# One hybrid decoder layer on one core: split remainders shared with GpSimd, a native first row, loaded bias tables, a new order

## The chip, the cores and the metric

The kernel runs on one core of a Trainium2 chip. The metric is the device time of one execution in microseconds, as the median of several runs. Three runs of the kernel before took 236.06, 235.83 and 234.94 us, so the median is 235.83 us. TensorE (PE) multiplies matrices and transposes, VectorE (DVE), ScalarE (ACT) and GpSimd (POOL) work on elements, and SyncE (SP) issues nearly all DMAs.

## The reference, cut to what matters

One layer of 256 tokens and 1024 channels. One projection by `w_in` (1024 x 5906) feeds four groups of six heads of width 64; each group's output is multiplied by its own SiLU gate; the four are joined, projected by `w_out` (1536 x 1024), and merged with a layer norm.

```python
proj = x @ w_in                       # split into the four groups' columns
y_a = moba_attention(a_q, a_k, a_v, slopes_moba) * silu(a_g)   # at 256 tokens: causal softmax with ALiBi
xbc = silu(causal_dw_conv(s_xbc))
y_b = rms_norm(ssd_mixer(xbc, s_dt, ...) * silu(s_z))          # Mamba-2 scan, dt = softplus(...)
y_c = dilated_attention(c_q, c_k, c_v, slopes_dil) * silu(c_g)
qkv = silu(causal_dw_conv(d_qkv))                              # q, k normalised
o_d = gated_delta_chunked(q, k, v, sigmoid(d_b), -exp(A) * softplus(d_a + bias))
y_d = rms_norm(o_d) * silu(d_g)
mix = concat([y_a, y_b, y_c, y_d]) @ w_out
out = layer_norm(2 ** 0.25 * x + mix)
```

## The kernel before

**Projections.** Every float32 weight tile is split (`split`, line 418) into a rounded part `whi` (ACT, float32r) and a remainder `wlo` = raw - whi (a subtraction on DVE, or on POOL where the running number of the split is in `POOL`, line 75: only number 6). The activations are split once into `xhi` and `xlo` (lines 469 to 472). A product is then three float32r matmuls, hi by hi, hi by lo and lo by hi, in this order within a tile, so the remainder is wanted last. There are 62 splits: 4 of the leading tiles `lead`, 46 of further `w_in` tiles and 12 of `w_out`. Tiles `raw`, `whi` and `wlo` have four buffers each, and SP issues the loads of `raw` in one queue. `channels` (line 495) computes columns with channels on partitions, `tokens` (517) with tokens on partitions, and `first_channels` (506) the first 512 columns while the input is still arriving, row block by row block, from `lead`.

**Stages.** The delta group comes first: conv k, gate d, `decays`, norm k, conv q, products `M` and `A`, conv v. Its triangular blocks are inverted on DVE by 62 small instructions on `Ub` (lines 785 to 789), whose results pass through DRAM; then join and delta. Beside it run gate s, conv bc, conv x, state and scan of the Mamba group, and the two attentions c and a. The output projection and the layer norm in two halves of 128 tokens come last. In `attention` (626), DVE adds a bias table to the scores and takes the maximum of a row, a small instruction multiplies it by -0.125 (line 646), and ACT takes the exponential with it as bias. DVE makes the table `biasc` (line 935) and ACT makes `biasa` (line 942), six instructions each, from loaded distances in `csb`. `softplus` (549) runs twice, once for each group.

**The order** of all instructions on all engines is written out by a planner in the kernel (class `Plan`): every call is recorded with an estimated cost, and a list scheduler picks the next by the length of the way to the end plus a priority of its stage (`PRIO`). `LIMIT` says how many of the eight PSUM banks a kind of use may hold. The engine wrapper gives DVE and POOL work on SBUF a shared resource `port`. All instructions are recorded at one helper line (356), so the profile tells them apart by tiles. Waits follow from the data.

Of the kernel before, what the change touches and what calls it, by code (L numbers as in the profile page):

```python
# [13 lines left out]
OP = mybir.AluOpType  # L14
# [41 lines left out]
NEAR = CAT["moba"][0]  # L56
# [4 lines left out]
SWITCH, PORT, AHEAD = 0.17, 0.9, {"dve": 0.015, "pe": 0.185}  # L61
# [5 lines left out]
PRIO = {"split": -6.8, "conv k": 1086.3, "gate d": -51.1, "decay d": 1000.2, "norm k": 1627.6, "conv q": 1480.8,  # L67
        "products": 1504.1, "norm q": 1768.9, "gate s": 323.3, "decay s": -1394.4, "values c": 263.3,
        "conv v": 246.6, "blocks": 124.5, "join": -297.8, "delta": 975.5, "conv bc": -546.4, "conv x": -369.3,
        "state": 595.2, "scan": 1273.9, "scores c": -1234.3, "attention c": 2093.1, "scores a": -183.7,  # L70
        "values a": -1630.5, "attention a": -481.0, "out": 94.7, "out 0": -1157.7, "out 1": -1399.5,
        "ln 0": -2309.4, "ln 1": 877.3}
CONST = -5, -4, -3
NRAW = 4
POOL = (6,)
POOLS = {"ps": (8, 512, F), "work": (3, W, F), "workd": (2, W, F), "workx": (1, W, F), "workg": (2, W, F), "cy": (3, S, F), "p": (3, W, F), "mx": (3, 4, F), "pt": (3, W, F), "oss": (2, 6, F), "sss": (2, 1, F), "srs": (2, 1, F)}
RINGS = {"raw": 4, "whi": 4, "wlo": 4}
LIMIT = {"pj": 5, "g": 6, "ed": 1, "es": 5, "n": 6, "m": 4, "d": 4, "o": 1, "td": 5, "b": 2, "s": 2, "ts": 4, "c": 6, "ct": 5, "cv": 6, "a": 4, "at": 1, "av": 1}
BEGIN, SLOW = 1.2, 2.5


class Plan:
# [69 lines left out]
    def add(self, eng, call, cost, outs, ins, dma=0.0, mode=None, port=False, place=None, slow=0.0):  # L152
# [5 lines left out]
        op = {"id": i, "bias": self.bias, "stream": self.stream, "eng": eng, "call": call, "cost": cost, "dma": dma,  # L158
# [41 lines left out]
    def run(self):  # L200
# [48 lines left out]
        while len(order) < len(ops):  # L249
# [22 lines left out]
            cost = o["cost"] * (0.5 if o["mode"] and o["mode"] == mode and o["place"] != place else 1.0)  # L272
# [94 lines left out]
def hybrid_layer(ctx, tc, plan, xT, x, w_in, w_out, convw, small, ln_g, ln_b, cst, out):  # L367
# [64 lines left out]
    rows, first, rest = [(slice(k, k + 1), slice(0, 512)) for k in range(2)], slice(0, 256), slice(256, 512)  # L432
    ws_lead = [split(w, rows if n else [(rows[0][0], first), (rows[0][0], rest), rows[1]]) for n, w in enumerate(lead)]
# [61 lines left out]
    def channels(c0, n):  # L495

        for j in range(n // 128):
            hi, lo = split(load(w_in, 0, KC, c0 + j * 128, 128))
            b = bank("pj")
            for n in range(3 * KC):  # L500
                p, k = n // KC, n % KC
                pj.matmul(b[:, :S], (lo if p == 2 else hi)[:, k, :], (xlo if p == 1 else xhi)[:, k, :],
                          start=n == 0, stop=n == 3 * KC - 1)
            yield j, b[:, :S]

    def first_channels():

        bs = [bank(t) for t in ("pj", "pj", "pj", "a")]
        for k in range(KC):
            hi, lo = ws_lead[k // 2]  # L510
            for p in range(3):
                for j in (0, 3, 1, 2):
                    pj.matmul(bs[j][:, :S], (lo if p == 2 else hi)[:, k % 2, (j * 128 + 128) % 512:][:, :128],
                              (xlo if p == 1 else xhi)[:, k, :], start=(k == 0 and p == 0), stop=(k == KC - 1 and p == 2))
        yield from enumerate(b[:, :S] for b in bs)

    def tokens(c0, n, raw=(), kinds=("pj", "pj")):

# [9 lines left out]
        for i in range(2):  # L528
            yield i, bs[i]
# [90 lines left out]
    def scores(m, cols, tag):  # L620
        qk[m] = new(m + "qk", 2, 3, S, tag=tag)
        for n in range(2):
            for j, b in channels(cols[n], W):
                act.activation(qk[m][:, n, j, :], b, AF.Copy)

    def attention(m, k0, bias, tag):
# [5 lines left out]
        for pr in range(3):  # L632

            ss, pts = [bank(m) for _ in halves], []
# [4 lines left out]
            for e, s_ in enumerate(ss):  # L639
                h = 2 * pr + e  # L640
                p, mx = new("p", W), new("mx", 2, 2)
# [16 lines left out]
                pts.append(pt)  # L658
            b = bank(m + "v")
# [85 lines left out]
    part("gate s")  # L745
    gz, raws = new("gz", 2, W), new("raws", 2, 6)
    for i, b in tokens(S_Z, NZ):
        gate(gz[:, i, :], b)
        dve.tensor_copy(raws[:, i, :], b[:, W:NZ])
    sdv, dt, sda = new("sdv", 2, 6), new("dt", 2, 6), new("sda", 2, 6)  # L750
    dve.tensor_add(sdv, raws, P("sdt")[:, None, :].to_broadcast([128, 2, 6]))
    softplus(sdv, dt)
    dve.scalar_tensor_tensor(sda, dt, -1.0, expA[:, 0:1, :].to_broadcast([128, 2, 6]), op0=OP.mult, op1=OP.mult)
# [64 lines left out]
    for i in range(2):  # L818
# [6 lines left out]
        for r in range(2):  # L825
            tp = slice(64 * r, 64 * r + 64)
# [11 lines left out]
        if i == 0:  # L838
# [95 lines left out]
    for h in range(NH):  # L934
        dve.scalar_tensor_tensor(bc[:, h, :], C("dil"), float(8 * SLOPES[h]), C("lnc"), op0=OP.mult, op1=OP.add)
# [5 lines left out]
    for h in range(NH):  # L941
        act.activation(ba[:, h, :], C("moba"), AF.Copy, scale=float(8 * SLOPES[6 + h]))
# [122 lines left out]
```

## Time and profile before

| what | us |
|---|---|
| median of three runs | 235.83 |
| the profiled execution | 235.13 |
| its span in the trace | 233.40 |
| PE busy | 221.6 |
| PE loading weights | 198.2 |
| DVE busy | 178.6 |
| ACT busy | 142.2 |
| POOL busy | 22.3 |

The profiled execution's time is 1.73 us longer than its span. A matmul's record covers its whole passage through the array, and the next one starts long before it ends, so PE can look busy across a short bubble. The row of weight loads (PEld) shows such bubbles better, as each matmul here has a load of its own.

### The profile page before, as it was taken

What the parts mean: (1) busy time and instruction counts of PE and PEld (TensorE: products, weight loads), DVE (VectorE), ACT (ScalarE), POOL (GpSimd) and SP (SyncE); (2) the same over time, 40 slices, a digit from 0 to 9 for tenths busy, and PEclk for the clock granted to TensorE, in tenths of its full rate; (3) what the DMA queues carried; (4) which work ended last, traced back from release to release, by engine and by line L of the source; (5) the groups of instructions that cost most, each with busy time, mean ns of one, the idle gap of its engine ahead of it and who ended that gap; (6) DMA issues with size and microseconds to landing.
All of it is one profiled execution on the core that took longest, in us unless ns stands there. A gap on an engine that the chain in (4) does not pass through costs nothing.

```text
span 233.4 us, 4547 instructions
## 1 busy us (share of the span) xinstructions
PE 221.6 (95%) x1679; PEld 198.2 (85%) x1679; DVE 178.6 (77%) x448; ACT 142.2 (61%) x300; POOL 22.3 (10%) x26
## 2 busy tenths in 40 slices
PE   7999999999999999899999999899999999999970
PEld 3999999699998999899888889697889988877870
DVE  2876999898869998899999996542579865464275
ACT  4777684656782544944669387999955547352210
POOL 3023020300020000000000000000023320000071
PEclk9999999999999999999999999999999999999997
DMA  6999627987550198666923524750525507550013
GB/s 177 357 368 325 186 84 200 272 215 212 144 152 14 18 262 237 172 183 179 260 79 81 145 73 128 192 161 4 176 94 183 179 4 246 204 180 3 0 67 113
DMA packets 45957, 36.92 MB, mean 158 GB/s; under 512 B 5600, under 2 KB 42592, under 8 KB 45936
## 3 DMA queue, kind: packets, MB, share of 16 engines
q1 hardware_dynamic: 45504, 36.25, 53.6%
q10 hardware_dynamic: 432, 0.39, 0.5%
q8 instruction: 13, 0.21, 0.3%
q14 instruction: 8, 0.07, 0.1%
HBM read 35.00 MB, written 1.64 MB: 157 GB/s over the span
## 4 chain that ended last, share of the span: by engine, by line
PE 42%; DVE 30%; DMA 11%; ACT 9%; issue 4%; SPq 2%; DVEq 0%; ACTq 0%
PE ps L356 42%; DVE wlo L356 10%; DMA raw<-in_w_in_dram 10%; DVE Ub L356 5%; DVE cy L356 4%; ACT whi L356 2%; DMA lead<-in_w_in_dram 2%; SPq L356 2%; DVE p L356 1%; DVE M L356 1%; DVE A L356 1%; ACT p L356 1%; ACT Ed L356 1%; DVE r L356 1%; ACT Tb L356 1%
## 5 line engine op out<-in xcount | busy, mean ns | idle before, releaser
L356 ACT ACTIVATE whi<-raw 128x1024 fp32r<-128x1024 f32 (+3 forms) x57 | 56.9, 1001 | 37.5 <-PE ps L356 25.6
L356 DVE TENSOR_TENSOR wlo<-raw,whi 128x1024 fp32r<-128x1024 f32 (+3 forms) x56 | 64.1, 1153 | 18.1 <-ACT whi L356 15.5
L356 PE MATMUL ps<-xhi,whi 128*128 128x256 f32 x272 | 42.0, 287 | 0.2 <-ACT whi L356 0.2
L356 PE MATMUL ps<-xhi,wlo 128*128 128x256 f32 x272 | 41.2, 285 | 0.0
L356 PE MATMUL ps<-xlo,whi 128*128 128x256 f32 x272 | 41.1, 285 | 0.0
L356 PEld LDWEIGHTS ps<-xhi,whi 128*128 128x128 f32 x272 | 35.8, 189 | 3.1 <-ACT whi L356 1.4
L356 PEld LDWEIGHTS ps<-xhi,wlo 128*128 128x128 f32 x272 | 35.7, 189 | 0.7 <-issue 0.7
L356 PEld LDWEIGHTS ps<-xlo,whi 128*128 128x128 f32 x272 | 35.7, 189 | 0.6 <-DVE xlo L356 0.2
L356 PE MATMUL ps<-whi,mix 128*128 128x512 f32 (+1 forms) x110 | 28.4, 349 | 0.0
L356 ACT ACTIVATE p<-p,mx 128x256 f32<-128x256 f32 (+1 forms) x48 | 19.6, 442 | 4.7 <-DVE mx L356 4.6
L356 PEld LDWEIGHTS ps<-whi,mix 128*128 128x128 f32 x110 | 19.2, 188 | 2.8
L356 DVE SCALAR_TENSOR_TENSOR cy<-ps,cw,cy 128x253 f32<-128x253 f32 (+2 forms) x48 | 19.9, 477 | 0.9 <-ACT cy L356 0.9
L356 PE MATMUL ps<-wlo,mix 128*128 128x512 f32 (+1 forms) x55 | 19.1, 353 | 0.0
L356 PE MATMUL ps<-whi,xlo 128*128 128x384 f32 (+2 forms) x64 | 17.6, 346 | 0.0
L356 PE MATMUL ps<-wlo,xhi 128*128 128x384 f32 (+2 forms) x64 | 17.1, 344 | 0.0
L356 PE MATMUL ps<-whi,xhi 128*128 128x384 f32 (+2 forms) x64 | 17.1, 345 | 0.0
L356 PEld LDWEIGHTS ps<-whi,xlo 128*128 128x128 f32 x64 | 11.5, 188 | 0.7 <-issue 0.7
L356 PEld LDWEIGHTS ps<-wlo,mix 128*128 128x128 f32 x55 | 10.3, 188 | 1.7 <-DVE wlo L356 0.4
L356 PEld LDWEIGHTS ps<-wlo,xhi 128*128 128x128 f32 x64 | 11.6, 188 | 0.0
L356 PEld LDWEIGHTS ps<-whi,xhi 128*128 128x128 f32 x64 | 11.3, 188 | 0.3 <-ACT whi L356 0.2
L356 POOL TENSOR_SCALAR_AFFINE_SELECT Es<-Es 128x1536 f32<-128x1536 f32 x1 | 1.5, 1548 | 101.2 <-ACT Es L356 101.2
L356 DVE TENSOR_TENSOR Ub<-BL,Ub 48x31 f32<-48x31 f32 (+15 forms) x31 | 10.3, 331 | 0.7
(226 smaller groups left out, 311.8 us busy)
## 6 DMA issues: line engine op xcount, KB each, us to landing
raw<-in_w_in_dram SPq DMA_DIRECT2D x30, 512.0 KB, 4.1
raw<-in_w_out_dram SPq DMA_DIRECT2D x12, 512.0 KB, 3.3
raw<-in_w_in_dram SPq DMA_DIRECT2D x8, 384.0 KB, 3.2
lead<-in_w_in_dram SPq DMA_DIRECT2D x7, 256.0 KB, 4.3
raw<-in_w_in_dram SPq DMA_DIRECT2D x4, 396.0 KB, 6.2
raw<-in_w_in_dram SPq DMA_DIRECT2D x4, 390.0 KB, 4.2
x<-in_x_dram SPq DMA_DIRECT2D x2, 512.0 KB, 3.7
xr<-in_xT_dram SPq DMA_DIRECT2D x7, 128.0 KB, 4.2
```

The lines of the kernel that those rows point to most:

```text
L356: self.plan.add(eng, lambda: f(*a, **k), cost, outs, ins, dma, mode, port or (eng == "pool" and not dma), place, slow)
```

## The change

It makes seven edits. (1) `POOL` lists 24 of the 62 splits: the remainders of lead tiles 2 and 3, one of gate d (as before), one of gate s, two of the c gates, all of conv v, three of conv bc, two of conv x, two of scores c, one of scores a, five of values a and two of `w_out` are subtracted on POOL. (2) The first of the eight row blocks in `first_channels` is multiplied as plain float32, in 4 matmuls instead of 12, straight from the loaded tiles, which need no split for it. (3) conv q and gate s are written ahead of one common softplus. (4) The bias tables are made on the host, with sign and scale, and loaded by two DMAs of 786 KB; the 12 instructions that made them go, and so does a load of 384 KB. (5) The scores take the factor -0.125 when ACT copies them out, DVE takes the minimum, and that is the exponential's bias as it is, so one DVE instruction a head goes. (6) The priorities and limits are new, and steps within a stage get priorities of their own (`STEPS`). (7) The planner counts matmuls beside each other at 0.63 or 0.75 of their cost instead of 0.5.

```diff
-LATE = ("moba", "dil", "lnc")
...
+def _biases():
+
+    dist = 128 + np.arange(128)[:, None] - np.arange(256)[None, :]
+    count = ((dist >= 0) & (dist <= 128)).astype(int) + ((dist >= 0) & (dist % 4 == 0)) \
+        + ((dist >= 0) & (dist % 16 == 0))
+    dil, moba = (np.where(m, -dist, -1e30).astype(np.float32)[:, None, :] for m in (count > 0, dist >= 0))
+    lnc = np.log(np.maximum(count, 1)).astype(np.float32)[:, None, :]
+    s1 = SLOPES[None, :, None]
+    return -np.concatenate([dil * s1[:, :6] + lnc, moba * s1[:, 6:]], 1).reshape(128, -1).astype(np.float32)
...
-SWITCH, PORT, AHEAD = 0.17, 0.9, {"dve": 0.015, "pe": 0.185}
+SWITCH, PORT, AHEAD = 0.17, 0.9, {"act": 0.037, "pe": 0.179}
...
-POOL = (6,)
+POOL = (2, 3, 6, 11, 18, 19, 21, 22, 23, 24, 26, 27, 28, 30, 31, 34, 39, 43, 44, 45, 46, 47, 53, 56)
...
+STEPS = {"conv q 1": {"dve": -80.5}, "products 4": {"dve": 16.7}, "values c 1": {"pe": -186.1},
...
-LIMIT = {"pj": 5, "g": 6, "ed": 1, "es": 5, "n": 6, "m": 4, "d": 4, "o": 1, "td": 5, "b": 2, "s": 2, "ts": 4, "c": 6, "ct": 5, "cv": 6, "a": 4, "at": 1, "av": 1}
+LIMIT = {"pj": 4, "g": 6, "ed": 6, "es": 4, "n": 4, "m": 6, "d": 5, "o": 2, "td": 1, "b": 1, "s": 4, "ts": 5, "c": 6, "ct": 6, "cv": 2, "a": 4, "at": 1, "av": 1}
+BESIDE = {(64, 128): 0.63, (128, 64): 0.75}
...
-    rows, first, rest = [(slice(k, k + 1), slice(0, 512)) for k in range(2)], slice(0, 256), slice(256, 512)
-    ws_lead = [split(w, rows if n else [(rows[0][0], first), (rows[0][0], rest), rows[1]]) for n, w in enumerate(lead)]
+    rows = [(slice(k, k + 1), slice(0, 512)) for k in range(2)]
+    ws_lead = [split(w, rows if n else rows[1:]) for n, w in enumerate(lead)]
...
-        sp.dma_start(csb[:, :NEAR], cst[:, :NEAR])
-        plan.after = loads[CONST[2]]
-        sp.dma_start(csb[:, NEAR:], cst[:, NEAR:])
+        sp.dma_start(csb, cst)
...
-            for p in range(3):
+            for j in (0, 3, 1, 2) if k == 0 else ():
+                pj.matmul(bs[j][:, :S], lead[0][:, 0, (j * 128 + 128) % 512:][:, :128], xr[:, 0, :], start=True, stop=False)
+            for p in range(3 if k else 0):
...
-                act.activation(qk[m][:, n, j, :], b, AF.Copy)
+                act.activation(qk[m][:, n, j, :], b, AF.Copy, scale=1.0 if n else -0.125)
...
-                                             scalar=-3e38, op0=OP.add, op1=OP.max, accum_out=mx[:, 0, n:n + 1])
-                dve.tensor_scalar(mx[:, 0], mx[:, 0], -0.125, None, op0=OP.mult)
+                                             scalar=3e38, op0=OP.add, op1=OP.min, accum_out=mx[:, 0, n:n + 1])
...
-                    act.activation(p[:, c], p[:, c], AF.Exp, bias=mx[:, 0, n:n + 1], scale=0.125,
+                    act.activation(p[:, c], p[:, c], AF.Exp, bias=mx[:, 0, n:n + 1], scale=-1.0,
...
+    beta, v2, dt2, g2 = new("beta", 2, 6), new("v2", 2, 2, 6), new("dt2", 2, 2, 6), new("g2", 2, 2, 6)
...
+    softplus(v2.rearrange("p m a b -> p (m a b)"), dt2.rearrange("p m a b -> p (m a b)"))
...
-    for h in range(NH):
-        dve.scalar_tensor_tensor(bc[:, h, :], C("dil"), float(8 * SLOPES[h]), C("lnc"), op0=OP.mult, op1=OP.add)
+    sp.dma_start(bc.rearrange("p h n -> p (h n)"), biases[:, 0:NH * 256])
...
-    for h in range(NH):
-        act.activation(ba[:, h, :], C("moba"), AF.Copy, scale=float(8 * SLOPES[6 + h]))
+    sp.dma_start(ba.rearrange("p h n -> p (h n)"), biases[:, NH * 256:])
```

## Rows read from the trace of the kernel before

**Rows 1.** Stretches: length, busy us (count) by engine, PE clock, DMA share, GB/s

```profile
4.84:23.50 18.66, 18.64 (x133) 18.08 (x133) 13.90 (x29) 14.15 (x28) 4.25 (x4) 1.00 1.05 346
23.50:69.20 45.70, 45.23 (x311) 42.28 (x311) 40.58 (x108) 31.22 (x63) 4.86 (x3) 1.00 0.68 183
69.20:136.00 66.80, 65.09 (x523) 60.30 (x521) 64.58 (x170) 38.01 (x79) 0.00 (x0) 1.00 0.56 146
143.40:173.30 29.90, 28.63 (x308) 24.73 (x307) 14.13 (x50) 29.02 (x76) 1.55 (x1) 1.00 0.52 147
173.30:226.40 53.10, 53.06 (x344) 44.92 (x344) 34.05 (x61) 21.93 (x39) 9.35 (x11) 1.00 0.34 114
226.40:233.40 7.00, 0.00 (x0) 0.00 (x0) 4.01 (x9) 0.00 (x0) 1.50 (x2) 0.76 0.32 112
```

**Rows 2.** Waits of PE's weight loads over the span: us, times, longest

```profile
PEld ps L356 <- issue: 4.8, 19, 0.4
PEld ps L356 <- ACT p L356: 2.2, 4, 1.2
PEld ps L356 <- DVE bcT L356: 1.6, 2, 1.0
PEld ps L356 <- DVE wlo L356: 0.8, 2, 0.4
PEld ps L356 <- ACT aqk L356: 0.5, 1, 0.5
```

**Rows 3.** Timeline of PE's weight loads: start, us, what, idle before and releaser

```profile
45.42 0.29 PEld L356 LDWEIGHTS ps<-kq,kT 64*128 64x128 f32 x2 [0.79 <-DVE gz L356]
...
56.19 0.52 PEld L356 LDWEIGHTS ps<-gdec,csb 128*128 128x128 f32 x4 [0.15 <-issue]
...
97.46 0.14 PEld L356 LDWEIGHTS ps<-csb,bcT 128*128 128x128 f32 x1 [1.02 <-DVE bcT L356]
...
151.72 0.31 PEld L356 LDWEIGHTS ps<-csb,p 128*128 128x128 f32 x3 [1.21 <-ACT p L356]
```

**Rows 4.** Timeline of the start: the first input, first weights, third row block

```profile
4.07 0.42 ACT L356 ACTIVATE xhi<-xr 128x256 fp32r<-128x256 f32 x1 [1.56 <-DMA xr<-in_xT_dram]
...
4.84 0.30 PEld L356 LDWEIGHTS ps<-xhi,whi 128*128 128x128 f32 x2 [1.11 <-ACT whi L356]
...
6.89 0.63 ACT L356 ACTIVATE whi<-lead 128x512 fp32r<-128x512 f32 x1 [0.67 <-DMA lead<-in_w_in_dram]
```

**Rows 5.** Timeline of PE: eight float32r matmuls; records of plain float32 matmuls

```profile
24.64 1.11 PE L356 MATMUL ps<-xlo,whi 128*128 128x256 f32 x8
...
105.18 0.94 PE L356 MATMUL ps<-bcT 128*128 128x128 f32 x6
```

**Rows 6.** Groups by shape: count, busy us, mean ns, idle before by releaser

```profile
L356 DVE TENSOR_TENSOR wlo<-raw,whi 128x1024 fp32r<-128x1024 f32 x41 | 49.8, 1221 | 14.7 <-ACT whi L356 12.2 <-PE ps L356 2.4 <-ACT pt L356 0.2
...
L356 DVE SCALAR_TENSOR_TENSOR sp<-sp 128x12 f32<-128x12 f32 x16 | 2.7, 169 | 0.4
...
L356 DVE SCALAR_TENSOR_TENSOR biasc<-csb 128x256 f32<-128x256 f32 x6 | 2.4, 422 | 0.2 <-DMA csb<-in_cst_dram 0.2
...
L356 ACT ACTIVATE biasa<-csb 128x256 f32<-128x256 f32 x6 | 2.0, 401 | 0.0
...
L356 DVE TENSOR_SCALAR mx<-mx 128x2 f32<-128x2 f32 x12 | 1.9, 162 | 0.1
...
L356 POOL TENSOR_TENSOR wlo<-raw,whi 128x792 fp32r<-128x792 f32 x1 | 1.9, 1901 | 0.5 <-ACT whi L356 0.5
```

**Rows 7.** One stretch, instructions on tile wlo alone: PE, PEld, DVE, POOL busy

```profile
69.20:136.00 66.80, 21.13 (x144) 18.38 (x142) 22.59 (x19) 0.00 (x0) 1.00 0.56 146
```

**Rows 8.** The same stretch, instructions on tile Ub alone: DVE, ACT, POOL busy

```profile
69.20:136.00 66.80, 15.13 (x44) 0.00 (x0) 0.00 (x0) 1.00 0.56 146
```

**Rows 9.** Timeline of POOL and DVE around 67 us: start, us, what

```profile
66.61 1.55 POOL L356 TENSOR_SCALAR_AFFINE_SELECT Ed<-Ed 128x1536 f32<-128x1536 f32 x1 [20.52 <-ACT Ed L356]
...
67.56 1.01 DVE L356 TENSOR_TENSOR kbg<-EQ,kq 128x384 f32<-128x384 f32 x1
68.61 0.56 DVE L356 TENSOR_TENSOR EQ<-EQ,kq 128x384 f32<-128x384 f32 x1
```

More of the change, by code (lines that the diff above doesn't have):

```diff
@@ L46, in _shape_constants @@
     at, n = {}, 0
-    for k, v in sorted(parts.items(), key=lambda kv: kv[0] in LATE):
+    for k, v in parts.items():
         at[k] = (n, v.shape[1])
@@ L66 @@
 HOLD = {10: (("hold_hi", "cvg", 1), ("hold_lo", "s3", 1))}
[L67 to L72, printed above, removed]
+PRIO = {"split": -6.8, "conv k": 1754.6, "gate d": -3686.9, "conv q": 2635.3, "gate s": 1971.9, "steps": 2405.1,
+        "decay d": 4610.2, "norm k": 2565.1, "products": 511.1, "norm q": 6509.2, "decay s": -1936.6,
+        "values c": 1236.9, "conv v": 564.7, "blocks": -849.3, "join": -1522.7, "delta": 2731.1,
+        "conv bc": 251.6, "conv x": -746.7, "state": -1080.7, "scan": 1994.8, "scores c": -1847.3,
+        "attention c": 5331.5, "scores a": 3428.1, "values a": -2729.5, "attention a": 874.0, "out": -399.9,
+        "out 0": -1772.1, "out 1": -3356.7, "ln 0": -815.9, "ln 1": -1491.2}
 CONST = -5, -4, -3
 NRAW = 4
-POOL = (6,)
+POOL = (2, 3, 6, 11, 18, 19, 21, 22, 23, 24, 26, 27, 28, 30, 31, 34, 39, 43, 44, 45, 46, 47, 53, 56)
 POOLS = {"ps": (8, 512, F), "work": (3, W, F), "workd": (2, W, F), "workx": (1, W, F), "workg": (2, W, F), "cy": (3, S, F), "p": (3, W, F), "mx": (3, 4, F), "pt": (3, W, F), "oss": (2, 6, F), "sss": (2, 1, F), "srs": (2, 1, F)}
 RINGS = {"raw": 4, "whi": 4, "wlo": 4}
-LIMIT = {"pj": 5, "g": 6, "ed": 1, "es": 5, "n": 6, "m": 4, "d": 4, "o": 1, "td": 5, "b": 2, "s": 2, "ts": 4, "c": 6, "ct": 5, "cv": 6, "a": 4, "at": 1, "av": 1}
+STEPS = {"conv q 1": {"dve": -80.5}, "products 4": {"dve": 16.7}, "values c 1": {"pe": -186.1},
[8 rows of a table added]
+         "attention a 6": {"act": -139.3}, "attention a 9": {"dve": 48.3, "act": -381.3},
+         "attention a 10": {"dve": 25.9}, "out 5": {"pe": 54.7}}
+LIMIT = {"pj": 4, "g": 6, "ed": 6, "es": 4, "n": 4, "m": 6, "d": 5, "o": 2, "td": 1, "b": 1, "s": 4, "ts": 5, "c": 6, "ct": 6, "cv": 2, "a": 4, "at": 1, "av": 1}
 BEGIN, SLOW = 1.2, 2.5
+BESIDE = {(64, 128): 0.63, (128, 64): 0.75}
 class Plan:
@@ L157, in add @@
         deps = {} if self.after is None else {self.after: 0.0}
-        op = {"id": i, "bias": self.bias, "stream": self.stream, "eng": eng, "call": call, "cost": cost, "dma": dma,
+        op = {"id": i, "bias": self.bias + STEPS.get(self.step, {}).get(eng, 0.0), "stream": self.stream, "eng": eng, "call": call, "cost": cost, "dma": dma,
               "mode": mode, "port": port, "place": place, "slow": slow, "deps": deps, "succ": [], "homes": []}
@@ L270, in run @@
                         turn[f["kind"]].pop(0)
-            cost = o["cost"] * (0.5 if o["mode"] and o["mode"] == mode and o["place"] != place else 1.0)
+            cost = o["cost"] * (BESIDE[o["mode"]] if o["mode"] in BESIDE and o["mode"] == mode and o["place"] != place else 1.0)
             clock[o["eng"]] = end = t + cost
@@ L366, in hybrid_layer @@
 @with_exitstack
-def hybrid_layer(ctx, tc, plan, xT, x, w_in, w_out, convw, small, ln_g, ln_b, cst, out):
+def hybrid_layer(ctx, tc, plan, xT, x, w_in, w_out, convw, small, ln_g, ln_b, cst, biases, out):
     nc = tc.nc
@@ L378, in part, with step @@
         plan.bias = PRIO.get(name, 0.0)
+        plan.stage = plan.step = name
+    def step(n):
+        plan.step = "%s %d" % (plan.stage, n)
     def new(name, *shape, dt=F, tag=None, bufs=1):
@@ L520, in tokens @@
         for k0 in range(0, KC, 2):
+            step(k0 // 2)
             hi, lo = split(raw[k0 // 2] if k0 // 2 < len(raw) else load(w_in, k0 * 128, 2, c0, n))
@@ L528, in tokens @@
         for i in range(2):
+            step(4 + i)
             yield i, bs[i]
@@ L549, in softplus @@
     def softplus(v, o):
-        t = new("sp", 6, 12)
-        ab, e, r, z, z2, p = (t[:, n, :].rearrange("p (a b) -> p a b", a=2) for n in range(6))
+        t = new("sp", 6, 24)
+        ab, e, r, z, z2, p = (t[:, n, :] for n in range(6))
         dve.scalar_tensor_tensor(ab, v, -1.0, v, op0=OP.mult, op1=OP.max)
@@ L632, in attention @@
         for pr in range(3):
+            step(4 * pr)
             ss, pts = [bank(m) for _ in halves], []
@@ L640, in attention @@
                 h = 2 * pr + e
+                step(4 * pr + e + 1)
                 p, mx = new("p", W), new("mx", 2, 2)
@@ L658, in attention @@
                 pts.append(pt)
+            step(4 * pr + 3)
             b = bank(m + "v")
@@ L680, in hybrid_layer @@
         dve.tensor_copy(rawd[:, i, :], b[:, W:ND])
-    beta, dav, gdec = new("beta", 2, 6), new("dav", 2, 6), new("gdec", 2, 6)
+    part("conv q")
+    for j, b in channels(D_Q, 256):
+        conv(7 + j, b, kq[:, j, :, 1, :])
+    part("gate s")
+    gz, raws = new("gz", 2, W), new("raws", 2, 6)
+    for i, b in tokens(S_Z, NZ):
+        gate(gz[:, i, :], b)
+        dve.tensor_copy(raws[:, i, :], b[:, W:NZ])
+    part("steps")
+    beta, v2, dt2, g2 = new("beta", 2, 6), new("v2", 2, 2, 6), new("dt2", 2, 2, 6), new("g2", 2, 2, 6)
     act.activation(beta, rawd[:, :, 0:6], AF.Tanh, scale=0.5)
     dve.tensor_scalar(beta, beta, 0.5, 0.5, op0=OP.mult, op1=OP.add)
-    dve.tensor_add(dav, rawd[:, :, 6:12], P("ddt")[:, None, :].to_broadcast([128, 2, 6]))
-    softplus(dav, gdec)
-    dve.scalar_tensor_tensor(gdec, gdec, -1.0, expA[:, 1:2, :].to_broadcast([128, 2, 6]), op0=OP.mult, op1=OP.mult)
+    for m, (r, n) in enumerate(((raws, "sdt"), (rawd[:, :, 6:12], "ddt"))):
+        dve.tensor_add(v2[:, m], r, P(n)[:, None, :].to_broadcast([128, 2, 6]))
+    softplus(v2.rearrange("p m a b -> p (m a b)"), dt2.rearrange("p m a b -> p (m a b)"))
+    for m in range(2):
+        dve.scalar_tensor_tensor(g2[:, m], dt2[:, m], -1.0, expA[:, m:m + 1, :].to_broadcast([128, 2, 6]), op0=OP.mult, op1=OP.mult)
+    dt, sda, gdec = dt2[:, 0], g2[:, 0], g2[:, 1]
     part("decay d")
@@ L723, in hybrid_layer @@
         for pr in range(3):
+            step(3 * i + pr)
             gb = [bank("m"), bank("m")]
@@ L743, in hybrid_layer @@
     dve.tensor_mul(qg, EQ, kq[:, :, 1, 1, :])
[L745 to L753, printed above, removed]
     part("decay s")
@@ L825, in hybrid_layer @@
         for r in range(2):
+            step(4 * i + r)
             tp = slice(64 * r, 64 * r + 64)
@@ L846, in hybrid_layer @@
                 dve.tensor_copy(St[q, :, e, :], b[q, :3 * HD].rearrange("p (k d) -> p k d", k=3))
+        step(4 * i + 2)
         ob = bank("o")
@@ L910, in hybrid_layer @@
         y = yd[:, i, :]
+        step(i)
         b = bank("s")
@@ L963, in hybrid_layer @@
         part("out")
+        step(kk)
         plan.after = gate_in
```

17 lines of the change are left out of this document (6 added, 11 removed), and 8 rows, old and new, of the table STEPS.

## The prediction

> **What bounds the kernel now.** I read the table of stretches first. From the first real weight load at 4.84 us to 226.40 us PE is busy almost without a break, at a granted clock of 1.00 (the 2.4 GHz level) throughout [rows 1]. So PE's stream of matmuls is the bound, and no edit here shortens that stream; one lengthens it a little. What can be won is the 4.84 us before it, the bubbles in it, and the 7.00 us after it [rows 1]. Next I read what PE's weight loads wait for, since a busy row of overlapping matmuls hides bubbles. The loads waited 4.8 us in 19 pieces for nothing that the profile names, and for named engines 2.2 us (softmax rows from ACT), 1.6 us (bcT from DVE), 0.8 us (remainders) and 0.5 us (aqk) in the larger entries [rows 2]; a further 0.79 us sits at 45.42, on DVE's gz [rows 3]. The timeline says where: bcT at 97.46, softmax mostly at 151.72 [rows 3]. Last I looked at who is full there. From 69.2 to 136.0 DVE is busy 64.58 of 66.80 us, and from 143.4 to 173.3 ACT is busy 29.02 of 29.90 us [rows 1]. These two stretches are PE-bound with a second engine close behind, so relief on that engine removes bubbles but can never return more than the bubbles: the named waits above add up to 2.2 + 1.6 + 0.8 + 0.5 + 0.79 = 5.9 us. That is the size to keep in mind when 27 us of DVE work are moved.
>
> **The remainders on POOL.** On DVE a remainder of 1024 columns takes 1.221 us; the one that POOL did took 1.901 us for 792 columns, by proportion 2.46 us for 1024 [rows 6]. Of the 24 listed splits 23 move: sixteen of 1024 columns, four of 768, one of 780, and two lead tiles of two rows of 512, in all 22,284 columns. DVE loses 22,284 x 1.19 ns = 27 us, POOL gains 22,284 x 2.40 ns = 53 us, spread over about 210 us. In the stretch 69.2 to 136.0 lie 19 remainders of 22.59 us [rows 7]. By the order of the stages they are those of conv v, conv bc, conv x and the two scores, splits 21 to 39, of which 11 are listed: DVE loses 11 x 1.22 = 13.4 us and POOL, idle there [rows 1], gets 11 x 2.46 = 27.0 us. Against this stands contention. At 67.56 DVE multiplied two SBUF tiles while POOL's select ran from 66.61 to 68.16, and took 1.01 us where the same shape just behind it took 0.56 us: 0.45 us lost for 0.60 us of overlap, or 0.75 [rows 9]. Work of DVE with two SBUF inputs in that stretch is 22.59 + 15.13 - 13.4 = 24.3 us after the move [rows 7, 8]; if it falls beside POOL by chance, 24.3 x 27.0 / 66.8 x 0.75 = 7.4 us are lost. DVE still comes out 6 us lighter, so of the bcT wait I take away three quarters: **-1.2 us**. The bound for contention goes from 0 to all 27 us of POOL's time; I price the chance collisions at **+0.3 us** of PE time, near the one row, as 6 us of slack take the rest.
>
> Each moved remainder also arrives 1.24 us later. Up to 173 us PE had no sizeable wait for one; both entries of 0.8 us are in the output projection, since the lo part is used last. Two of the twelve `w_out` remainders move, 2 x 1.24 = 2.5 us later in sum, about a fifth of it uncovered as two of the stretch's eleven were waited for [rows 2]: **+0.5 us** (0 to +2.5). Behind a remainder POOL's own steps now queue, the powers of the norms and the two selects: DVE's cb, oss and the products M wait for those, up to 2.46 us each. The projection stream covers them in four stretches; if it doesn't, it is the second rival. SP's loads wait for remainders to free `raw`, but four buffers and a DMA share of 0.34 to 0.68 after 23.5 us [rows 1] leave room: 0.
>
> **The first row in float32.** PE starts 4.84 us in, after ACT made whi; x landed at 4.07 [rows 4]. Without that step PE starts up to 0.4 us earlier. Twelve float32r matmuls at (1.11 - 0.285) / 7 = 0.118 us are 1.42 us, with 0.285 us as the length of one record; plain float32 has two records for each matmul, at (0.94 - 0.275) / 5 = 0.133 us for 128 columns, so four of 256 columns cost about 8 x 0.266 = 2.1 us [rows 5] (1.7 if the second half of a record is cheaper). The third row block still lands at 6.89 and needs 0.63 us of ACT [rows 4], so PE can't pass that block's start before about 7.8, where the old order reached it near 8.1. I take **-0.2 us** (-0.5 to +0.4).
>
> **One softplus, made after gate s.** It saves 16 small DVE instructions, 16 x 0.169 = 2.7 us, and biasc saves 6 x 0.422 = 2.5 us [rows 6], mostly before 69 us, where DVE is busy 40.58 of 45.70 us [rows 1]. The decays of the delta group now wait for gate s too, but gz was being finished at 45.42 and gdec was used only at 56.19 [rows 3], so this wait adds nothing. The gz wait should go: **-0.8 us** (0 to -0.8).
>
> **Minimum and loaded tables.** The minimum saves 0.162 us of DVE in each of 12 heads [rows 6], on the chain from scores to softmax; outside the long one that chain cost PE 2.2 - 1.2 = 1.0 us [rows 2, 3], half of it **-0.5 us**. The table biasa cost ACT 6 x 0.401 = 2.4 us [rows 6] in the stretch where ACT is full, just ahead of the first softmax of group a, which PE then awaited for 1.21 us, and beside aqk, awaited for 0.5 us [rows 2, 3]. With 2.4 us less in front both go: **-1.7 us** (0 to -1.7). The two DMAs of 786 KB take 2.3 us each at the 346 GB/s of the first stretch. If the first is issued there, where the DMA share is 1.05, it delays weights by 2.3 us less the 1.1 us of the 384 KB that go; later the share is at most 0.68 [rows 1] and it is hidden. The second needs the tile that the triangular inverse frees, and what is queued on SP behind it is the way of the inverse through DRAM. Up to 2.3 us later for that chain; attention and projections cover it. Both 0 (to +1.2 and +2.3).
>
> **New order.** The 4.8 us of unnamed bubbles stand mainly where matmuls of 32 and 64 rows alternate with the full ones. A new order can save part of them or add some; nothing in the trace says which: 0 (-2.4 to +2.4). The tail of 7.00 us is the same instructions: 0.
>
> **The sum:** -1.2 + 0.3 + 0.5 - 0.2 - 0.8 - 0.5 - 1.7 = -3.6 us. Against the profiled execution (span 233.40 + 1.73 = 235.13) that is 231.5; that execution lies 0.7 us under the median of the runs, 235.83, against which it is 232.2. I forecast the middle, **231.8 us**.
>
> **Rivals.** *More is won* (226.9 us): all named waits of 5.9 us go, the start gives 0.5 and half of the unnamed bubbles, 2.4, go with the new order: -8.8 us, 226.3 to 227.0. For it: every one of these waits is on DVE or ACT where something is lifted. Against: bubbles at mode changes need not care for DVE.
>
> *Waits are replaced* (235.3 us): the 23 late remainders, or steps queued behind them on POOL, cost PE about 0.15 us each, 3.5 us. For it: 1.24 us is more than any slack that the loads' waits prove. Against: almost no wait for a remainder up to 173 us. That POOL relieves an engine which isn't the bound is the same case.
>
> *Slower, by the port* (237.5 us): from 69.2 to 136.0 the 27.0 us of POOL block DVE at the rate of the one row, 0.75 x 27.0 = 20.3 us, instead of 7.4. DVE gains 13.4, saves 6 x 0.162 = 1.0 on its heads, and had 2.2 us free, so from 16.6 us of blocking on the stretch grows: +3.7 us. The gz, bcT and half-softmax gains are then lost; -0.2 - 1.7 + 0.5 remain. 235.13 + 3.7 - 1.4 = 237.4, or 238.1 by the median; I put 237.5. For it: remainders left on DVE and the inverse both read two SBUF tiles, so a DVE that is kept full will often stand at such an instruction. Against: half of DVE's work there reads PSUM, and the planner holds the two apart. The Trainium skill speaks for this rival: its page "SBUF — State Buffer", section "Who interferes with whom", says that a VectorE instruction with two SBUF inputs contends with a GpSimd instruction that reads SBUF, and that the loser waits for the whole instruction. The loss of 0.45 of 0.60 us agrees nearly [rows 9]; by the rule taken to its end all 27.0 us would block, and the stretch would grow by 10.4 us.
>
> **How the numbers follow.** Forecast 0.50, more won 0.17, replaced 0.18, slower 0.15. About 0.5% is what a measurement of this kernel can tell from no change, 1.2 us: faster means under 234.65. Faster: 0.50 + 0.17 and a sixth of the replaced case, 0.70. Same: most of the replaced case, 0.14. Slower: the port and the rest, 0.16. The forecast's own range is 229.5 to 234; for 8 in 10 the range reaches down to the case of more won and up to near the port's, 226.8 to 237.
>
> **What would show it.** In the trace after: POOL with about 53 us more and remainders near 2.4 us; DVE near 140 us plus what is blocked; the two-input rows of DVE (remainders, Ub) longer than 1.22 and 0.35 us if the port bites. The waits for gz, bcT and aqk should be gone, and the first plain matmuls should start near 4.4 us. Wrong would be: PE's loads waiting on POOL's remainders by more than 2 us, DVE still full in the middle, or unnamed bubbles that changed by more than 2 us.

## The result and the profile after

The changed kernel takes 237.78 us in the median of nine runs (236.60 to 238.96), the kernel before 235.79 in nine: a ratio of 1.008 with an interval of 1.0052 to 1.0108. It is slower by 0.8%, where 231.8 us and "faster" were forecast; the time lies above the range too. The profiled execution took 236.63 us, with a span of 234.9. One of the six executions of e2 below (266.57 us at a mean clock of 0.753) was in a slow state of the chip and counts in no figure.

First the stretches of after (length, then busy us and count of PE, PEld, DVE, ACT, POOL, the clock, DMA share, GB/s), to be read against [rows 1]:

```profile
23.50:69.20 45.70, 45.29 (x320) 43.29 (x319) 37.13 (x97) 32.05 (x64) 20.33 (x10) 1.00 0.64 174
69.20:136.00 66.80, 62.63 (x517) 59.23 (x515) 60.50 (x149) 40.62 (x89) 21.07 (x9) 1.00 0.62 158
```

In the middle stretch VectorE now has 6.3 us free, where it had 2.2, and still TensorE is busy only 62.63 us of the same length, where it was 65.09. The waits of its weight loads (us, times, longest), against [rows 2], say on what:

```profile
PEld ps L375 <- DVE vT L375: 3.3, 1, 3.3
PEld ps L375 <- ACT p L375: 3.0, 5, 1.3
PEld ps L375 <- issue: 1.8, 7, 0.4
...
PEld ps L375 <- DVE yd L375: 1.0, 1, 1.0
PEld ps L375 <- ACT TZ L375: 0.9, 1, 0.9
```

The waits for bcT, gz, aqk and remainders are gone, and the unnamed ones fell from 4.8 to 1.8 us. Against that stands one wait of 3.3 us, which the kernel before hasn't got. The timelines of DVE, POOL and PEld, from 73 to 84 us (start, us, what, idle before and releaser), show it whole:

```profile
74.14 0.48 DVE L375 SCALAR_TENSOR_TENSOR cy<-ps,cw,cy 128x255 f32<-128x255 f32 x1
74.53 1.77 DVE L375 SCALAR_TENSOR_TENSOR vT<-vT,cy 128x256 f32<-128x256 f32 x1
...
78.53 2.23 DVE L375 SCALAR_TENSOR_TENSOR vT<-vT,cy 128x256 f32<-128x256 f32 x1
80.68 2.41 DVE L375 SCALAR_TENSOR_TENSOR cy<-ps,cw,cy 128x254 f32<-128x254 f32 x5
83.01 0.42 DVE L375 SCALAR_TENSOR_TENSOR vT<-vT,cy 128x256 f32<-128x256 f32 x1
...
73.62 2.40 POOL L375 TENSOR_TENSOR wlo<-raw,whi 128x1024 fp32r<-128x1024 f32 x1 [0.29 <-ACT whi L375]
77.72 2.76 POOL L375 TENSOR_TENSOR wlo<-raw,whi 128x1024 fp32r<-128x1024 f32 x1 [1.70 <-ACT whi L375]
...
83.48 0.64 PEld L375 LDWEIGHTS ps<-csb,vT 128*128 128x128 f32 x6 [3.29 <-DVE vT L375]
```

The three rows of vT are the closing multiplies of `conv` for the delta group's values. Undisturbed, one takes 0.42 us (83.01). The first two began while POOL was at a remainder, and ended 0.28 us after it, both times: 1.35 + 1.81 = 3.16 us long over. The taps `cy<-ps,cw,cy` read PSUM and pass beside POOL at their usual pace (74.14). All stand in one chain on VectorE, which has no idle time from 72.7 to 83.4 us, and whose end TensorE awaited for 3.29 us.

### The profile page after: what moved, and what is told of

Read it like the earlier page. It is cut to its first block, busy times and chain, and to the rows that moved or that the text cites. A ratio compares the mean times of both kernels' runs of the same rounds, so it can differ in the third digit from the quotient of the medians.

```text
span 234.9 us, 4502 instructions
## 1 busy us (share of the span) xinstructions
PE 218.7 (93%) x1675; PEld 199.3 (85%) x1675; DVE 165.8 (71%) x387; ACT 138.6 (59%) x291; POOL 75.4 (32%) x51
## 4 chain that ended last, share of the span: by engine, by line
PE 51%; DVE 21%; DMA 11%; ACT 10%; issue 4%; POOL 1%; SPq 1%; DVEq 0%; ACTq 0%
PE ps L375 51%; DMA raw<-in_w_in_dram 7%; DVE wlo L375 5%; DVE cy L375 4%; DMA lead<-in_w_in_dram 4%; ACT whi L375 3%; ACT p L375 3%; DVE yd L375 2%; DVE vT L375 2%; ACT Es L375 2%; DVE mix L375 1%; POOL wlo L375 1%; DVE r L375 1%; DVE Es L375 1%; DVE work L375 1%
## 5 line engine op out<-in xcount | busy, mean ns | idle before, releaser
L375 ACT ACTIVATE whi<-raw 128x1024 fp32r<-128x1024 f32 (+3 forms) x57 | 56.1, 1000 | 38.4 <-PE ps L375 17.6
L375 POOL TENSOR_TENSOR wlo<-raw,whi 128x1024 fp32r<-128x1024 f32 (+3 forms) x22 | 51.1, 2329 | 79.9 <-ACT whi L375 51.9
L375 DVE TENSOR_TENSOR wlo<-raw,whi 128x1024 fp32r<-128x1024 f32 (+3 forms) x35 | 41.6, 1192 | 21.6 <-ACT whi L375 21.2
L375 PE MATMUL ps<-xhi,whi 128*128 128x256 f32 x268 | 43.0, 289 | 0.5 <-ACT whi L375 0.5
L375 PE MATMUL ps<-xhi,wlo 128*128 128x256 f32 x268 | 40.0, 283 | 0.0
L375 PE MATMUL ps<-xlo,whi 128*128 128x256 f32 x268 | 39.3, 283 | 0.0
L375 PEld LDWEIGHTS ps<-xlo,whi 128*128 128x128 f32 x268 | 34.8, 188 | 0.3 <-issue 0.2
L375 DVE SCALAR_TENSOR_TENSOR cy<-ps,cw,cy 128x253 f32<-128x253 f32 (+2 forms) x48 | 22.0, 478 | 3.4 <-ACT cy L375 2.9
L375 PE MATMUL ps<-whi,xhi 128*128 128x384 f32 (+2 forms) x64 | 17.8, 348 | 0.0
L375 PE MATMUL ps<-wlo,xhi 128*128 128x384 f32 (+2 forms) x64 | 16.6, 340 | 0.0
L375 DVE TENSOR_TENSOR Ub<-BL,Ub 48x31 f32<-48x31 f32 (+15 forms) x31 | 14.0, 451 | 0.8
```

The lines of the kernel that those rows point to most:

```text
L375: self.plan.add(eng, lambda: f(*a, **k), cost, outs, ins, dma, mode, port or (eng == "pool" and not dma), place, slow)
```

## The experiments

Theory 1: the port. The loss is the time by which POOL's remainders hold up two-SBUF-input instructions of VectorE, where TensorE waits for these. Rivals: the new order, the other four edits, or POOL's load as such. The edits are shown abridged. The kernel before, timed beside each set of runs, took 235.79 to 236.34 us in the median; each ratio is to the one beside it. "Order kept" means that the order was planned for the changed kernel (in e3 and e4 for the kernel before) and the edit made in it.

### e1: the two remainders made quiet

```diff
+ if count in (27, 28):   # 8 columns subtracted, then two fills, 1.9 us
+     nc.gpsimd.tensor_sub(lo[:, :, 0:8], src[:, :, 0:8], hi[:, :, 0:8])
+     for _ in range(2): nc.gpsimd.memset(f32(lo[:, :, 8:]), 0.0)
```

> The changed kernel with the order of every engine kept. The remainders of splits 27 and 28, the two that ran on POOL at 73.62 and 77.72 us beside the two late vT steps of DVE, are replaced on POOL by work of about the same length that reads no SBUF: a subtraction of 8 columns and two fills with zeros (so these two remainders are left out of the product). Theory 1, the port: DVE's vT steps read two SBUF tiles and were blocked (1.77 and 2.23 us instead of 0.42), so both come back to 0.42 us, PE's wait of 3.29 us for vT goes, and the time falls by 2.5 to 3.5 us against the changed kernel, to 0.990 to 0.997 of the kernel before. Theory 2, the order: PE's queue holds vT's transposes too early whoever computes what, so the wait stays above 2 us and the time stays at 1.005 to 1.011. If the dips of the granted clock in some executions (0.982 to 0.988 beside 0.994) come from that long wait, the clock is 0.993 or more in every run here.

233.44 us, ratio 0.9867 (0.9821 to 0.9914). The vT steps took 413 ns each, the wait at 80 us was gone, with the order of after kept, so the order alone doesn't make it. Two instructions on an engine that is idle two thirds of the time were worth 4.3 us, more than the wait of 3.3; e10 tells why. The granted clock was 0.990 to 0.995, where 0.993 or more was expected in every run; none fell to the 0.982 to 0.988 of the five slower executions of the changed kernel.

### e2 and e9: the two remainders on VectorE

```diff
- (pool if count in POOL else dve).tensor_sub(...)
+ (pool if count in POOL and count not in (27, 28) else dve).tensor_sub(...)
```

> The changed kernel with the order kept, the same two remainders subtracted on DVE at their places in the order. Theory 1, the port: DVE pays 2 x 1.22 = 2.4 us for them in place of 1.36 + 1.81 = 3.2 us of blocking, so PE's wait for vT is shorter but not gone, 1.5 to 2.8 us, and the time lies 0.5 to 1.8 us below the changed kernel. Theory 2, the order: no difference, wait above 3 us. A rival within theory 1: DVE stands idle elsewhere in this stretch, so the two fit into idle time and the wait goes altogether.

240.34 us, 1.0176 (1.012 to 1.0233): a miss, 2.6 us above the changed kernel. The same kernel again, for its profile:

> The same edit as in the run that put the two remainders before the vT steps on VectorE (240.7 us), one look for its profile; nothing left out. Theory 1: two subtractions of 1.21 us now stand in VectorE's own order in front of the last vT step, 2.4 us where the blocked steps had lost 3.17, so TensorE still waits for vT at 80 us, 1.5 to 3 us, and the rest of the 240.7 is a stretch after that wait in which the granted clock is low. Rival: TensorE does not wait for vT there, and the time is lost elsewhere (later remainders, a PSUM bank freed late).

239.99 us. PEld and the two subtractions that are new in VectorE's order:

```profile
75.89 1.02 PEld L376 LDWEIGHTS ps<-xhi,whi 128*128 128x128 f32 x8 [1.52 <-DVE A L376]
85.22 1.15 PEld L376 LDWEIGHTS ps<-csb,vT 128*128 128x128 f32 x6 [3.47 <-DVE vT L376]
...
73.57 1.23 DVE L376 TENSOR_TENSOR wlo<-raw,whi 128x1024 fp32r<-128x1024 f32 x1 [1.26 <-ACT whi L376]
...
80.92 1.22 DVE L376 TENSOR_TENSOR wlo<-raw,whi 128x1024 fp32r<-128x1024 f32 x1
82.05 1.51 DVE L376 SCALAR_TENSOR_TENSOR cy<-ps,cw,cy 128x253 f32<-128x253 f32 x3
83.48 1.69 DVE L376 SCALAR_TENSOR_TENSOR vT<-vT,cy 128x256 f32<-128x256 f32 x1
```

So the chain in front of vT has no room for two subtractions either: they cost 2.45 us and a wait for whi of 1.26 us, and POOL, early now with its next remainder, still held the last vT step. The place is wrong, whoever does them.

### e5: the closing multiply reads PSUM

```diff
- act.activation(o, y, AF.Tanh)
- dve.scalar_tensor_tensor(o, o, 1.0, y, op0=OP.add, op1=OP.mult)
+ th = bank[:, S:2 * S]              # unused half of the block's own PSUM bank
+ act.activation(th, y, AF.Tanh)
+ dve.scalar_tensor_tensor(o, th, 1.0, y, op0=OP.add, op1=OP.mult)
```

> The changed kernel with its order and every one of GpSimd's remainders kept; in conv, tanh is written to the unused upper half of the channel block's own PSUM bank, so that VectorE's closing multiply reads one operand from PSUM and one from SBUF, where it read two from SBUF. Nothing of the computation is left out. Theory 1 (the shared port: the two vT multiplies that took 1.77 and 2.23 us beside GpSimd's remainders, where one takes 0.42, are 3.17 us of the 3.29 us that TensorE stood at 80 us): both fall to about 0.45 us with GpSimd as busy as before, TensorE's wait at 80 us goes, and the kernel takes 233.4 to 234.8 us, 3 to 4 below the changed kernel's 237.8. Theory 2 (the run with two quiet GpSimd instructions won because GpSimd moved less data at all, not because of what VectorE reads): GpSimd moves as much as in the changed kernel, the wait stays, 237 to 238 us.

233.68 us, 0.9891 (0.9864 to 0.9919): 4.1 us below the changed kernel and 1.1% below the kernel before, with the same 24 remainders on POOL. DVE, POOL, PEld:

```profile
74.36 0.41 DVE L375 SCALAR_TENSOR_TENSOR vT<-ps,cy 128x256 f32<-128x256 f32 x1
...
77.28 0.41 DVE L375 SCALAR_TENSOR_TENSOR vT<-ps,cy 128x256 f32<-128x256 f32 x1
...
73.48 2.40 POOL L375 TENSOR_TENSOR wlo<-raw,whi 128x1024 fp32r<-128x1024 f32 x1 [0.32 <-ACT whi L375]
77.66 2.41 POOL L375 TENSOR_TENSOR wlo<-raw,whi 128x1024 fp32r<-128x1024 f32 x1 [1.78 <-ACT whi L375]
...
80.41 0.64 PEld L375 LDWEIGHTS ps<-csb,vT 128*128 128x128 f32 x6 [0.27 <-DVE vT L375]
```

The step at 74.36 lies inside POOL's remainder and takes 0.41 us. POOL's load is unchanged, so load as such is out; what counts is where VectorE's second operand comes from. The Trainium skill, "SBUF — State Buffer", section "Who interferes with whom", states just this: two SBUF inputs contend with a GpSimd instruction that reads SBUF; at most one, outside VectorE's 2-port modes, doesn't. The trace agrees with both halves, 1.77 and 0.41 us.

### e11: no remainder on POOL reads SBUF for long

e5, with the edit of e1 for all 24 splits.

> The kernel with tanh through PSUM (233.7 us), and each of GpSimd's 24 split remainders replaced by a subtraction of 8 columns and two fills that read no SBUF and take about 1.9 us; the remainders' product is so left out of the result for those 24 splits. Order kept. It takes away the 12 us by which VectorE's instructions still run long beside GpSimd. Theory 1 (only a collision on a chain that TensorE waits for costs; that is left at the gate of the scan, 0.7 us, and in the solve, 3.6 us of VectorE in front of waits of 0.7, 0.5 and 0.6 us): 231.9 to 233.0 us. Rival (every blocked microsecond is lost): 221 to 223 us. Rival (nothing is left to win, the other collisions are all covered): 233.4 to 234.0 us.

230.27 us, 0.9753 (0.9723 to 0.9783): 3.4 below e5, where 0.7 to 1.8 were expected. Of the 12 us by which VectorE ran long in e5, and of all else that the edit changes, 3.2 reached the end. Both traces have 1675 matmul records on the same tiles in the same order, so the gap can be read as it grows, in the time of e5: -0.07 us at 45, 0.43 at 46, 0.99 at 55.5, 1.32 at 58, 1.61 at 81, 2.36 at 120, 2.48 at 147, 3.19 at the last. Each step stands at a weight load that waits longer in e5. The first three:

```profile
45.87 0.19 PEld L375 LDWEIGHTS ps<-xhi,whi 128*128 128x128 f32 x1 [0.55 <-ACT whi L375]
...
55.21 1.00 PEld L375 LDWEIGHTS ps<-xhi,whi 128*128 128x128 f32 x8 [0.51 <-ACT whi L375]
...
57.32 0.77 PEld L375 LDWEIGHTS ps<-rowsd,selR 128*128 128x128 f32 x6 [0.28 <-DVE rowsd L375]
```

The two waits for `whi`, 1.0 us together, are not VectorE's. In e5 ScalarE had itself waited for the weights (1.10 us at 44.77, 0.66 at 52.21), and in e11 it hadn't. The load that it awaited at 52.21 went out at 48.36 us, when a remainder on POOL gave up its `raw` buffer; in e11, where the subtraction of 8 columns does that, it went out at 45.31. SP's waits for POOL over the whole span, first e5, then e11:

```profile
SPq L375 <- POOL wlo L375: 57.4, 20, 7.3
```

```profile
SPq L376 <- POOL wlo L452: 30.6, 16, 6.4
```

The wait at 57.32 is for `rowsd`, which stands on VectorE behind a remainder that POOL held up; e5, then e11:

```profile
55.20 1.63 DVE L375 TENSOR_TENSOR wlo<-raw,whi 128x1024 fp32r<-128x1024 f32 x1 [1.50 <-ACT whi L375]
...
57.30 1.78 DVE L375 TENSOR_TENSOR cd<-rk,exd 128x6 f32<-128x6 f32 x1
```

```profile
53.98 1.23 DVE L376 TENSOR_TENSOR wlo<-raw,whi 128x1024 fp32r<-128x1024 f32 x1 [0.76 <-ACT whi L376]
...
55.68 0.17 DVE L376 TENSOR_TENSOR cd<-rk,exd 128x6 f32<-128x6 f32 x1
```

With its 0.34 us and the later steps (0.29 us at vT, 0.75 at mx behind a blocked Ub, 0.74 at yd) contention makes 2.1 of the 3.2 us. The multiply of six columns lost 1.61 us and cost nothing, as the gap does not grow between 58 and 80 us. The size of the blocked instruction doesn't matter, only whose way it stands in. The 3.3 us lost on xlo at the start and the 1.6 us of the solve at 136 us cost TensorE almost nothing either. That the first wait for `whi` (0.50 us) has the same cause as the second is argued: its load went out only 0.17 us later, but behind one that POOL had delayed by 1.58.

### e10: a pause without contention

```diff
+ if ct == 13:                       # e5, last of the three vT steps: eight times, not once
+     for _ in range(8): dve.scalar_tensor_tensor(o, th, 1.0, y, ...)
```

> The kernel with tanh through PSUM (233.7 us), and its last vT multiply done nine times over instead of once (the same values each time; about 0.40 us each, one PSUM operand, so nothing of it is blocked): a pause for TensorE of about 3.2 us at 80 us, without any contention. Nothing left out. Theory 1 (a pause costs its length): 236.6 to 236.9 us, granted clock 0.99 and over in all executions. Theory 2 (a pause of that length also lets TensorE's clock fall behind it in some executions, as it did in the execution of the changed kernel with the split first row): 237.2 to 238.5 us, with a mean granted clock under 0.99 in about half of the executions.

238.30 us, 1.0085 (1.0054 to 1.0116), 4.6 us above e5. The step ran eight times, not the nine of the expectation (3.62 us in all). Matmuls behind the pause, and stretches:

```profile
83.69 1.29 PE L375 MATMUL ps<-csb,vT 128*128 128x128 f32 x6 [3.53 <-DVE vT L577]
84.63 1.84 PE L375 MATMUL ps<-xhi,whi 128*128 128x256 f32 x7
...
84.00:87.00 3.00, 3.00 (x17) 3.00 (x15) 2.16 (x6) 0.00 (x0) 0.00 (x0) 0.50 0.66 174
...
90.00:95.00 5.00, 5.00 (x45) 5.00 (x44) 3.87 (x10) 3.15 (x6) 2.40 (x1) 1.00 0.48 120
```

Behind the pause the granted clock is 0.50 (1.2 GHz) for some 3 us, then 1.00 again (2.4 GHz). Against e5, record by record, TensorE is 3.28 us later at the first matmul behind the pause and 4.83 us later at 92 us: the clock adds 1.55. Theory 2 holds; the mean clock was low in all six executions (0.975 to 0.988), not in half of them. The changed kernel does the same in some executions: four of its nine, with a mean clock of 0.994 to 0.995, took 236.6 to 237.2 us, the five with 0.982 to 0.988 took 237.8 to 239.0. The profiled one was of the first kind, so its trace shows only the wait. Nor does it take such a stop: in e7's profile, below, the clock is 0.50 from 165.5 to 168.9 us, with no wait of a weight load over 0.65 us in the 10 us before. Why the clock falls in one execution and not in the next stays open.

### e6 and e8: the first row split again

```diff
- pj.matmul(bs[j], lead[0][:, 0, ...], xr[:, 0, :], start=True)          # 4, float32
+ for p in range(3): nc.tensor.matmul(bs[j], (lo if p == 2 else hi)[:, 0, ...], (xlo if p == 1 else xhi)[:, 0, :], ...)
```

> The changed kernel with its order kept, and the first row of the projection split into hi and lo again (12 fp32r matmuls and the conversions of row 0, as in the kernel before), the rest as changed. Theory 1 (the native row loses at the start: in the profiled execution its eight records took 0.427 us each at the low clock and TensorE was through the second row block 0.74 us later than before): 0.5 to 0.9 us below the changed kernel, 236.9 to 237.3 us. Theory 2 (the start is bounded by the loads of the later rows, and the row's form is hidden): within 0.3 us of the changed kernel, 237.5 to 238.1 us.

238.68 us, 1.01 (1.0064 to 1.0136), not told apart from the changed kernel: theory 2, though the median lies beyond either span. Its profile had the slow clock behind the wait, slice 15 of the 40 in the page's row:

```profile
PEclk9999999999999959999999999999999999999996
```

> The two edits of the runs before together on the changed kernel (tanh through PSUM, first row split again), and the delta rule's output scaled inside its PSUM bank, so that its multiply with the gate has one PSUM operand too; order kept, nothing left out. Theory 1: the two gains add, 3 to 4 and 0.5 to 0.9 us: 232.6 to 234.2 us, below the kernel before as well (235.8). Theory 2 (one wait takes the place of the other): no better than the better of the two alone, 234 to 235 us.

234.95 us, 0.9946 (0.9922 to 0.997): better than before, not better than e5. It also scales the delta rule's output inside its PSUM bank, so three edits stand in it. In its profile POOL began a remainder at 74.53 us, 1.05 us later than in e5, and one left on VectorE met it, in front of vT, for which TensorE waited 1.86 us:

```profile
75.43 2.59 DVE L375 TENSOR_TENSOR wlo<-raw,whi 128x1024 fp32r<-128x1024 f32 x1 [0.25 <-ACT whi L375]
```

Where two instructions meet hangs on a microsecond upstream, here on when ScalarE had made whi.

### e3, e4 and e7: the other edits without the remainders

e3 puts the native first row into the kernel before, e4 the tables and the minimum, each in the order of before. e7 is the changed kernel with `POOL = (6,)`, planned anew.

> The kernel before with its order kept, only the first row block multiplied as plain float32 (4 matmuls in place of 12, its split not made). My prediction: PE starts 0.4 us earlier and reaches the third row block 0.2 us earlier, time -0.2 us. Theory from the trace after: the eight records ran at 0.427 us each while the clock had not risen yet, so PE reaches the second row block at about 7.2 instead of 6.37 us and the third at 8.8 instead of 8.08, and the whole stream follows: +0.6 to +0.9 us, 1.003 of the kernel before.

> The kernel before with its order kept, only the bias tables loaded by two DMAs (the late part of csb not loaded) and the minimum taken as the exponential's bias. My prediction: the wait of 1.21 us for softmax at 151.72 and that of 0.5 us for aqk go, half of the other softmax waits, -1.7 - 0.5 = -2.2 us, 0.991 of the kernel before. Rival: the wait at 151.72 stays above 0.8 us because ACT is still full with exponentials and splits (in the changed kernel the same group waited 1.34 us with its table loaded), time 0 to -0.8 us.

> The changed kernel with only split 6 on GpSimd, as before, and the order planned anew; all other edits and all weights of the order stay. Theory 1 (the remainders on GpSimd cost more, through blocked VectorE instructions, than VectorE's freed time is worth, and the other edits are worth little): the time falls to the kernel before's or a little under, 234.5 to 236.5 us. Theory 2 (the new order and the other edits lose the time, and the remainders on GpSimd are a gain that hides part of it): it rises over the changed kernel, 238 to 241 us, as the run with the two remainders on VectorE did.

e3: 236.53 us, 1.0018 (0.9987 to 1.0048); e4: 235.94, 1.0007 (0.9974 to 1.004). Neither differs from no change. e7: 235.80, 0.9971 (0.9944 to 0.9998): the four other edits with an order of their own are worth 0.7 us, at the edge of the noise. Six of its twelve executions had a clock of 0.983 to 0.985 and took 1.1 us more than the others in the median. Why e4 wins nothing, in its PEld rows, to be held against [rows 3]:

```profile
93.54 0.14 PEld L368 LDWEIGHTS ps<-csb,bcT 128*128 128x128 f32 x1 [1.18 <-DVE bcT L368]
...
148.84 0.30 PEld L368 LDWEIGHTS ps<-whi,xhi 128*128 128x128 f32 x2 [0.82 <-DVE mx L368]
152.09 0.31 PEld L368 LDWEIGHTS ps<-csb,p 128*128 128x128 f32 x3 [1.39 <-ACT p L368]
```

The softmax wait is as long as before (1.39 for 1.21), and the aqk wait of 0.5 has given way to one of 0.82 for mx.

## Why the prediction was wrong, by its steps

**The remainders, contention (+0.3 us forecast): the step that failed.** The amount was nearly right. I expected 7.4 us of blocking from 69.2 to 136 us; the trace has 1.35 + 1.81 on vT, 0.44 on bcT, 0.47 on a remainder and 2.09 + 0.35 on Ub, 6.5 us. VectorE came out 4.1 us lighter (64.58 to 60.50) for 6 forecast; with the 2.2 us that it had free before, 6.3 were free, about the slack that I counted on. Wrong was "6 us of slack take the rest". Slack of an engine over a stretch is not slack of each chain on it: 3.16 us fell on one chain between two TensorE stages, and 2.9 us of it arrived at the end (the gap between after and e5 in the same matmul record is 0.07 us at 69 us, 3.07 at 83 and 3.01 at the last). The row to ask was which two-SBUF instructions TensorE awaits next, and those were readable before: vT's close, bcT's close, yd.

**SP's loads (0): failed too.** I wrote that four `raw` buffers and a low DMA share leave room. SP's queue waited 57.3 us for POOL's remainders in after; most of that costs nothing, but in e5 against e11 late weights cost TensorE 1.0 us.

**The clock (no term).** I had no term for what TensorE's clock does behind a stop. It is 1.55 us in e10, and about 1.2 us in five of nine runs of the changed kernel.

**The rival "slower, by the port"** gave 237.5 us, near the 237.8 measured, by another way: it wanted 16.6 us of blocking to fill VectorE, and VectorE never filled. Its time was right by chance, its resource was right, its point of decision wrong.

**Relief (-1.2), gz (-0.8).** Both waits went. What the relief is worth when POOL holds nothing up is read from e11 against e7: 230.3 to 235.8, 5.5 us. That is rough: the two have different orders, e11's fills are shorter than remainders, and half of e7's executions have the low clock. The remainders on POOL took all of it back and more, 7.5 us: 4.1 by the convs' closing multiplies, the clock behind them included (after to e5), and 3.4 elsewhere (e5 to e11), about two thirds by contention and one third by late loads.

**Late remainders (+0.5).** No load waits for one in after; that was nothing.

**First row (-0.2).** Mis-sized, and hidden by 10 us, where after and e5 are 0.09 us apart. I priced the row at 2.1 us from records at full clock. It took 3.13 us in after, whose trace has its first record of a granted clock, of 1.00, only at 6.94 us, and 1.89 in e3, where it begins at 3.76. What else holds the second row block is its weights, which ScalarE gets only when they land. ScalarE, in after, in e6 and in e4 (native, split, split in the old order):

```profile
5.91 0.63 ACT L375 ACTIVATE whi<-lead 128x512 fp32r<-128x512 f32 x1 [1.60 <-DMA lead<-in_w_in_dram]
```

```profile
6.01 0.63 ACT L375 ACTIVATE whi<-lead 128x512 fp32r<-128x512 f32 x1 [1.04 <-DMA lead<-in_w_in_dram]
```

```profile
6.17 0.63 ACT L368 ACTIVATE whi<-lead 128x512 fp32r<-128x512 f32 x1 [1.26 <-DMA lead<-in_w_in_dram]
```

TensorE reached that block at 7.22 (behind the slow row), 7.00 and 7.16 us. In the profiled execution of before these weights landed early (conversion at 5.29, block at 6.37), and from that one execution [rows 4] I had priced the start.

**Minimum and tables (-0.5, -1.7).** Failed: e4 measures 0 for 2.2. I took a wait as gone because work was taken out ahead of it. The row said who released the load, not what ScalarE had waited for; in after and e4 the same softmax loads wait 1.34 and 1.39 us.

**New order (0, -2.4 to +2.4).** The unnamed waits fell by 3.0 us, past the bound; in their place came named ones (TZ 0.9, yd 1.0, softmax 0.8 more).

**What would show it.** POOL's 53 us more came exactly (75.4 for 22.3), remainders of 2.4 us too. VectorE without blocking is about 151 us (e11), not 140. Of the marks for "wrong" I named loads that wait on POOL's remainders; the true mark was a load that waits on a VectorE instruction which waited on POOL. The mark of unnamed bubbles (a change of over 2 us) came as well, as a gain.

## What to carry to other kernels

Before work is moved to GpSimd, list VectorE's instructions with two SBUF inputs that TensorE will wait for, and those that stand in front of them, however small, and charge each with up to a whole GpSimd instruction (1.1 to 2.1 us on the larger ones here); slack summed over the stretch doesn't pay for it. Ask too which loads wait for a buffer that the slower engine now frees. Putting one operand into a spare half of a PSUM bank took the port out of the matter and turned 0.8% slower into 1.1% faster. Allow for the clock behind a stop of TensorE: 1.55 us behind one of 3.5 us in e10, about 1.2 in some executions of the changed kernel and none in others.

## What the runs showed of the hardware

A 128x6 multiply of 0.17 us took 1.78 us beside a GpSimd subtraction. GpSimd is held up as well: where VectorE's 1.21 us subtraction was under way (77.01), the next remainder took 2.76 us for 2.40. ScalarE's tanh of 128x256 was no slower into PSUM than into SBUF: 379 ns on average, against 413 (vT) and 407 (bcT). A plain float32 matmul of 256 columns has two records; at after's start they began 0.43 us apart until 6.57 us and 0.22 from 6.97, in e3 0.22 throughout. After's first record of a granted clock begins at 6.94 us and e3's at 3.76, both at 1.00 (2.4 GHz); the windows print 1.00 before it as well, where there is no record. That the level before it is the half one (1.2 GHz) is read from the spacing. Over the twelve traces of executions at full clock that first record begins anywhere from 3.76 to 6.98 us.
